# Three sums moved to transfers or to another place: the gates' T, the squares of h2, and the last pair of the down projection

## The chip, the cores and the metric

The kernel runs on one core of one Trainium2 chip. The metric is the device time of one execution in microseconds. Before the change the median of 3 runs is 2573.82 us (2573.16 to 2576.52).

The engines by the names of the profile: PE (TensorE, matrix products, with its weight loads PEld), DVE (VectorE), ACT (ScalarE), POOL (GpSimd) and SP (SyncE, which only issues transfers here). Each has its own queue of instructions and works them off in order; an instruction that waits holds all that stand behind it. SP, ACT and POOL also issue transfers (DMA).

## What is computed

One layer of a hybrid encoder on 512 tokens of 2048 numbers, in float32:

```python
u = rms_norm(h, mix_pre_g)
q, k, v, ca, cb, ga, gb = split(u @ w_in)
y_attn = neighbourhood_attention(q, k, v, rpb) @ w_attn_o
y_conv = conformer_conv(ca, cb, ...)
merged = sigmoid(ga) * y_attn + sigmoid(gb) * y_conv
h = h + rms_norm(merged @ w_out, mix_post_g)
u = rms_norm(h, ffn_pre_g)
gate, up = split(u @ w_gate_up)
f = (silu(gate) * up) @ w_down
h = h + rms_norm(f, ffn_post_g)
```

## The kernel before

**Tiles.** Everything is kept transposed: a tile has 128 features on the partitions and the 512 tokens along the row. The stream of 2048 features is 16 such tiles (KT = 16; HT = 8 is half of them). Tokens are also taken in halves, A and B, of 256. A tile of 128x512 float32 is 256 KB; most live in one pool of 66 slots (`slot`).

**Products.** TensorE's reduced float32 is used three times for one product: each operand is split into hi (a cast on ACT) and lo (what is left, a subtraction on DVE), and hi·lo, hi·hi and lo·hi are added (`gemm`, `interleaved`). Weights come in chunks of 512 KB: `wchunk` loads `raw_*` (SP, a pool of five buffers with the tag "raw"), casts it to `whi_*` (L126, ACT) and subtracts to `wlo_*` (L127, DVE), with three buffers each.

**Strassen pairs.** Most gates (gemms g2 to g15), the feed-forward's products (f5 and later) and a part of the down projection (d0 to d14) use the Winograd form of Strassen's algorithm: `strassen` takes two tiles of outputs at once, makes seven products of half size from four quarters of the weights (`g2q` and so on, also in the "raw" pool; `s1` has its own buffer and is summed by an accumulating transfer from POOL), and needs the activations as b11, b21, b22 and as sums T1 to T4 (`winograd_t`, `winograd_tt`). Its three sums x, y, z stand in PSUM banks: of `bank` (four) or `abank` (four more), in turn, by the parity of its last argument.

**Stage A, from g0 to g2** (L535 to L587). `u` is the normalized stream, 16 tiles as hi and lo. The gemm g0 makes the first two gates in four banks pg; it is a loop over c = 0 to 7 with one weight chunk each. In the same loop the operands of the Strassen pairs are made: SP copies halves of u's hi and lo into tiles b (six copies of 128 KB for each c, L552 and L553), `un` = hi + lo is summed (L547: one tile on POOL, one on DVE), `winograd_tt` makes `tt` from it on DVE, and `merged` splits tt (L148 a cast on ACT, L149 a subtraction on DVE). After the loop ACT takes four sigmoids of pg (L566), and the pairs i = 2 to 15 follow, where `strassen(..., i)` puts g2 on `bank`, that is on the banks of pg.

**Stage B, the second residual** (L666 to L734). `h2` makes the new stream tile by tile on DVE (L676, L677, L679); each tile is squared on ACT and added up by `sumsq` (L338), here on POOL. Meanwhile `interleaved` runs the gemm f0 on u_2, 8 chunks of 24 matmuls. Then `rstd` sums the squares over the partitions with small matmuls (r_s, L294), takes the power on POOL (L304), and `by_column` spreads the result over the partitions (r_b, L311); r3 is the copy of it on ACT (L699). A gemm of four chunks follows (two more columns of f0). All of the next stage on DVE starts from r3: L705 and L706 (the gated products of f0), L719 (the stream times r3) and the operands b and T of the following pairs. TensorE runs f1 in the meantime, 16 steps of 24 matmuls on halves (`plain`).

**Stage C, the down projection** (L829 to L855). Eight Strassen pairs; the results are joined on DVE (L284), multiplied by a row on POOL (L841) and added to y_d in DRAM by an accumulating transfer (L842). POOL's queue also issues the loads `ad*` (L758) of the activations that the last gemm, pd1, takes.

**The order.** A scheduler puts each engine's instructions in order when the kernel is built, by its own estimates and by the pools; `tc.keep_in_program_order` and `load_in_order` pin single ones.

Of the kernel before, what the change touches and what calls it, by code (L numbers as in the profile page):

```python
# [25 lines left out]
F32 = mybir.dt.float32  # L26
F32R = mybir.dt.float32r
AF = mybir.ActivationFunctionType
ALU = mybir.AluOpType
# [37 lines left out]
def hybrid_block(ctx: ExitStack, tc, xT, vecs, rpb, mask, w_c0, w_qk, w_v, w_gg, w_cg, w_ao, w_co, w_out, w_g0, w_gu, w_dn, outT):  # L67
# [264 lines left out]
    def sumsq(acc, x, name, last=False, eng=nc.vector):  # L332

        sq = slot(f"{name}_sq")
        nc.scalar.activation(sq, x, AF.Square)
        if acc is None or last:
            return (acc or []) + [sq]
        eng.tensor_tensor(out=acc[0], in0=acc[0], in1=sq, op=ALU.add)  # L338
        return acc

    def col(c, i):
# [73 lines left out]
            conv(i, pc[2 * i], pc[2 * i + 1])  # L415

    un = []

    def normalize(c):

        for k, t in enumerate(x_pair(c, f"xn{c}"), 2 * c):
            t2 = slot(f"un{k}")
            nc.vector.scalar_tensor_tensor(out=t2, in0=t, scalar=col(C_PRE, k), in1=r1, op0=ALU.mult, op1=ALU.mult)
            un.append(split(t2, f"un{k}"))

    rate = R_CONV
# [109 lines left out]
    pg = [bank(f"g0_{n}") for n in range(4)]  # L536
    for c in range(HT):
        hi, lo = wchunk(w_gg[c], f"g0_{c}")
        un = stp.tile([P, 2, NT], F32, tag="S", name=f"un{c}")
        for j, k in enumerate((c, c + HT)):  # L540
            ah, al = u[k]
            for n, ps in enumerate(pg):
                s = slice((j * 4 + n) * P, (j * 4 + n + 1) * P)
                nc.tensor.matmul(ps, hi[:, s], al, start=c + j == 0, stop=False)
                nc.tensor.matmul(ps, hi[:, s], ah, start=False, stop=False)
                nc.tensor.matmul(ps, lo[:, s], ah, start=False, stop=c + j == HT)
            (nc.gpsimd, nc.vector)[j].tensor_tensor(  # L547
                out=un[:, j], in0=ah.bitcast(F32), in1=al.bitcast(F32), op=ALU.add
            )
            blocks = [slot(f"b{j}{c}_{n}") for n in range(1 + j)]  # L550
            for t, cols in zip(blocks, (A, B)):
                nc.sync.dma_start(t[:, A], ah[:, cols].bitcast(F32))  # L552
                nc.sync.dma_start(t[:, B], al[:, cols].bitcast(F32))  # L553
# [19 lines left out]

    op = operands(b11, b2, t12, t34)
    for i in range(2, KT):
        c11, c12, c21, c22 = strassen(w_cg[2 * CT + i], w_cg[2 * CT + KT + i], op, f"g{i}", i)
        if i == KT - 1:
            ya = [load_ya(h) for h in range(YA_EARLY)]
        ga, gb = slot(f"ga{i}"), slot(f"gb{i}")
        joined(ga[:, A], c11)  # L580
        joined(ga[:, B], c12)
        nc.scalar.activation(ga, ga, AF.Sigmoid)
        nc.scalar.dma_start(g_d[i], ga)
        joined(gb[:, B], c22)
# [82 lines left out]
    a_d = dr.tile([FT, P, NT], F32, name="a_d")  # L667


    acc, u, w = None, [], []  # L670
    pf = [bank(f"f0_{n}") for n in range(4)]

    def h2(i, cols):
# [9 lines left out]
    for c in (*range(SPLIT), *range(HT)):  # L683
# [6 lines left out]
        for i in (2 * c, 2 * c + 1):  # L690
            h2(i, cols)
            if cols != A:
                nc.scalar.dma_start(h_d[i], f[i])
                acc = sumsq(acc, f[i], f"h{i}", last=i == KT - 1, eng=nc.gpsimd)
        if c == HT - 1:
            r = rstd(acc, D, "r3", pin=True)
        interleaved(pf, *w[c], u, c, cols)
    r3 = slot("r3")
    nc.scalar.copy(r3, by_column(r, "r3", pin=True))  # L699
    pf += [abank(f"f0_{n}") for n in range(4, 6)]  # L700
    gemm([(pf[4 + n], w_gu[n * FT + 2]) for n in range(2)], u, "f0")
    for j in range(3):
        t = stp.tile([P, 2, NT], F32, tag="S", name=f"sg{j}")
        t, up = t[:, 0], t[:, 1]
# [122 lines left out]


    op = operands(b11, b2, b_t12, b_t34)  # L829
    for o in range(0, KT, 2):  # L830
        if o == KT - 2:
            acts = [load(DN_S + k) for k in range(EARLY)]
# [1 line left out]
        c11, c12, c21, c22 = strassen(w0, w1, op, f"d{o}", o // 2)  # L834
        if o == KT - 2:
            acts += [load(DN_S + k) for k in range(EARLY, EARLY + MORE)]
        for i, (ca, cb) in enumerate(((c11, c12), (c21, c22))):
            t = slot(f"ys{o + i}")
            joined(t[:, A], ca)
            joined(t[:, B], cb)  # L840
            nc.gpsimd.tensor_tensor(out=t, in0=t, in1=irow, op=ALU.mult)  # L841
            nc.gpsimd.dma_start(y_d[o + i], t, accum_op=ALU.add)  # L842


    y = [None] * KT
# [1 line left out]
    for g in range(KT // 2 - 1):  # L847
        outs = [((bank, abank)[g % 2](f"pd1_{o}"), o) for o in (2 * g, 2 * g + 1)]
        for _, o in outs:
            y[o] = slot(f"y{o}")  # L850
            load_in_order(y[o], y_d[o])
        gemm([(ps, w_dn[o, :, DN_S * P :]) for ps, o in outs], acts, f"wd1_{g}", n=DN_R, more=lambda k: load(DN_S + k), pin=g < 2)
        for ps, o in outs:
            nc.vector.tensor_tensor(out=y[o], in0=ps, in1=y[o], op=ALU.add)  # L854
            acc = sumsq(acc, y[o], f"y{o}")  # L855
# [155 lines left out]
```

## The time and the profile before

| | before |
|---|---|
| median of 3 runs | 2573.82 us |
| the profiled execution, its own time | 2575.59 us |
| its span | 2573.8 us |
| granted TensorE clock, mean | 0.992 |
| PE busy | 2520.9 us, 98% |
| DVE busy | 1884.2 us, 73% |
| ACT busy | 1121.9 us, 44% |
| POOL busy | 355.8 us, 14% |
| bytes moved | 421.42 MB, mean 164 GB/s |

Times in the profile are microseconds from the start of the span. A row of the waits reads: the engine and line that waited, what it waited for, then the total, the number of times and the longest. A row in order of time reads: start, duration, engine, line, operation, output<-inputs, shape, how many together, and in brackets the idle time ahead with what ended it. A row of windows has the length of the window and then, for PE, PEld, DVE, ACT and POOL, the busy time with the number of instructions, and at its end the granted clock, the transfers' share of the 16 DMA engines, and GB/s. A row of groups has the busy time, the mean of one in ns, and the idle time ahead. A row of transfers has the issuing queue, the number, the size of each and the median time from issue to landing. The tile names lack their running number.

### The profile page before, as it was taken

The page shows a single profiled execution, that of the slowest core. Times are in us where ns is not written, and L with a number is a line of the kernel's source. Part 1 is how long each engine was busy: PE and PEld are TensorE (multiplying, and loading weights), DVE is VectorE, ACT ScalarE, POOL GpSimd, SP SyncE. Part 2 cuts the span into 40 slices and gives each one's busy share as a digit, 9 for nine tenths or more (in the row PEclk, how much of TensorE's full clock was granted, in tenths as well). Part 3 has the DMA queues.
Part 4 walks back from the last instruction along what each step waited for, and adds up shares of the span by engine and source line. Part 5 has one row for each costly group of instructions (what it writes and reads, how often), then busy time and mean ns, then how long its engine had stood idle before and what let it go on. Part 6 is the DMA issues. An engine that isn't in the chain of part 4 may idle for free.

```text
span 2573.8 us, 34661 instructions
## 1 busy us (share of the span) xinstructions
PE 2520.9 (98%) x13235; PEld 2163.8 (84%) x13235; DVE 1884.2 (73%) x2394; ACT 1121.9 (44%) x1644; POOL 355.8 (14%) x363
## 2 busy tenths in 40 slices
PE   9999999989999999998999999999999999989997
PEld 8888888878888888888898888888888878878887
DVE  5999896687775655338888888788888888863235
ACT  5223333355554422224455555555555565442222
POOL 0110222210000011003201111112120012230002
PEclk9999999999999999999999999999999999999999
DMA  6234323566667335224356665667666577773335
GB/s 208 93 126 150 109 92 108 156 209 185 183 194 245 136 127 193 95 98 150 117 152 172 178 182 172 176 204 213 195 193 195 168 244 198 185 243 112 115 114 164
DMA packets 143367, 421.42 MB, mean 164 GB/s; under 512 B 16608, under 2 KB 30048, under 8 KB 143200
## 3 DMA queue, kind: packets, MB, share of 16 engines
q1 hardware_dynamic: 106880, 326.42, 38.4%
q0 software_dynamic: 19040, 62.40, 11.8%
q10 hardware_dynamic: 17280, 30.38, 3.2%
q8 instruction: 104, 1.70, 0.3%
q14 instruction: 63, 0.52, 0.1%
HBM read 367.76 MB, written 45.09 MB: 160 GB/s over the span
## 4 chain that ended last, share of the span: by engine, by line
PE 91%; DVE 4%; DMA 2%; issue 2%; ACT 1%; POOL 1%; SPq 0%; DVEq 0%; ACTq 0%; POOLq 0%
PE f L246 19%; PE f L248 10%; PE g L246 7%; PE d L246 4%; PE g L248 3%; PE pd L172 3%; PE pd L176 3%; PE pd L175 3%; PE po L176 2%; PE po L172 2%; PE po L175 2%; PE qk L176 2%; PE qk L175 2%; PE qk L172 2%; PE py L172 2%; PE py L176 2%
## 5 line engine op out<-in xcount | busy, mean ns | idle before, releaser
L386 DVE SCALAR_TENSOR_TENSOR cv<-z,vec,cv 128x497 f32<-128x497 f32 (+14 forms) x240 | 190.8, 797 | 4.7
L127 DVE TENSOR_TENSOR wlo_wd<-raw_wd,whi_wd 128x1024 fp32r<-128x1024 f32 (+1 forms) x58 | 62.2, 1077 | 106.4 <-ACT whi_wd L126 105.2
L127 DVE TENSOR_TENSOR wlo_wo<-raw_wo,whi_wo 128x1024 fp32r<-128x1024 f32 x36 | 47.5, 1318 | 106.9 <-ACT whi_wo L126 106.8
L126 ACT CAST whi_wd<-raw_wd 128x1024 fp32r<-128x1024 f32 (+1 forms) x58 | 54.0, 934 | 157.5 <-PE pd L175 107.4
L126 ACT CAST whi_wo<-raw_wo 128x1024 fp32r<-128x1024 f32 x36 | 37.9, 1054 | 130.0 <-PE po L175 122.7
L304 POOL TENSOR_TENSOR r_r<-r_v,mhalf 128x2 f32<-128x2 f32 (+1 forms) x6 | 6.7, 1125 | 473.4 <-DVE r_v L302 473.4
L126 ACT CAST whi_y<-raw_y 128x1024 fp32r<-128x1024 f32 x32 | 33.5, 1052 | 83.5 <-PE py L175 79.4
L126 ACT CAST whi_qk<-raw_qk 128x1024 fp32r<-128x1024 f32 x32 | 33.6, 1051 | 77.1 <-PE qk L175 56.5
L127 DVE TENSOR_TENSOR wlo_qk<-raw_qk,whi_qk 128x1024 fp32r<-128x1024 f32 x32 | 40.5, 1264 | 32.1 <-ACT whi_qk L126 32.0
L627 DVE TENSOR_TENSOR gg<-py,gg 128x512 f32<-128x512 f32 x32 | 21.8, 690 | 55.7 <-PE py L176 55.7
L127 DVE TENSOR_TENSOR wlo_y<-raw_y,whi_y 128x1024 fp32r<-128x1024 f32 x32 | 53.3, 1670 | 12.5 <-ACT whi_y L126 11.3
L745 POOL TENSOR_TENSOR asum<-asum,asq 128x512 f32<-128x512 f32 x15 | 20.2, 1347 | 242.9 <-ACT asq L744 242.9
L172 PE MATMUL py<-ycl,whi_y 128*128 128x512 f32 x128 | 49.8, 389 | 0.0
L175 PE MATMUL py<-ych,whi_y 128*128 128x512 f32 x128 | 49.8, 389 | 0.0
L176 PE MATMUL py<-ych,wlo_y 128*128 128x512 f32 x128 | 49.8, 389 | 0.0
L788 ACT ACTIVATE sg<-sg 128x512 f32<-128x512 f32 x39 | 24.7, 634 | 51.6 <-DVE sg L284 51.6
L465 POOL TENSOR_TENSOR bm<-braw,msk 128x128 f32<-128x128 f32 x56 | 41.9, 781 | 15.9 <-DMA braw<-in_rpb 15.9
L769 POOL TENSOR_TENSOR an<-an,asum 128x512 f32<-128x512 f32 x16 | 27.8, 1735 | 102.6 <-DMA an<-a_d 100.6
L854 DVE TENSOR_TENSOR y<-pd,y 128x512 f32<-128x512 f32 x14 | 9.7, 692 | 41.4 <-PE pd L176 41.4
L841 POOL TENSOR_TENSOR ys<-ys,irow 128x512 f32<-128x512 f32 x16 | 27.4, 1715 | 85.6 <-DVE ys L284 42.7
L637 POOL TENSOR_TENSOR gg<-gg,gg 128x512 f32<-128x512 f32 x16 | 20.6, 1287 | 115.0 <-ACT whi_y L126 73.5
L156 PE MATMUL f<-b,wlo_f 128*128 128x256 f32 x128 | 36.3, 283 | 0.0
(3074 smaller groups left out, 8552.8 us busy)
## 6 DMA issues: line engine op xcount, KB each, us to landing
raw_wd<-in_w_dn SPq DMA_DIRECT2D x42, 512.0 KB, 3.6
raw_wo<-in_w_out SPq DMA_DIRECT2D x36, 512.0 KB, 3.8
raw_qk<-in_w_qk SPq DMA_DIRECT2D x32, 512.0 KB, 3.8
a_d<-sg ACTq DMA_DIRECT2D x44, 256.0 KB, 3.7
raw_v<-in_w_v SPq DMA_DIRECT2D x16, 512.0 KB, 3.7
raw_y<-in_w_ao SPq DMA_DIRECT2D x16, 512.0 KB, 3.7
gg<-g_d SPq DMA_DIRECT2D x32, 256.0 KB, 4.3
raw_y<-in_w_co SPq DMA_DIRECT2D x16, 512.0 KB, 3.6
```

The lines of the kernel that those rows point to most:

```text
L126: cast(hi[:, s], raw[:, s])
L127: nc.vector.tensor_tensor(out=lo[:, s], in0=raw[:, s], in1=hi[:, s].bitcast(F32), op=ALU.subtract)
L156: nc.tensor.matmul(o, lo, t[:, A], start=False, stop=last, skip_group_check=True)
L172: mmul = nc.tensor.matmul(ps, hi[:, s], al, start=first, stop=False)
L175: nc.tensor.matmul(ps, hi[:, s], ah, start=False, stop=False)
L176: nc.tensor.matmul(ps, lo[:, s], ah, start=False, stop=last)
L246: nc.tensor.matmul(ps, hi[:, ws[k]], t, start=first and k == 0, stop=False, skip_group_check=True)
L248: nc.tensor.matmul(ps[:, A], lo[:, ws[k]], t[:, A], start=False, stop=last and k == HT - 1, skip_group_check=True)
L386: nc.vector.scalar_tensor_tensor(out=a[:, to], in0=z[:, fr], scalar=col(C_WDW, i * CW + w), in1=a[:, to], op0=ALU.mult, op1=ALU.add)
L465: nc.gpsimd.tensor_tensor(out=bm[:, o + i - i0], in0=raw[:, :, i * BC : (i + 1) * BC], in1=msk[:, o + i - i0, None, :].broadcast_to([P, RO ...
L769: nc.gpsimd.tensor_tensor(out=t, in0=t, in1=arow, op=ALU.mult)
L841: nc.gpsimd.tensor_tensor(out=t, in0=t, in1=irow, op=ALU.mult)
```

## The change

1. `normalize` also writes each of the 16 normalized tiles to DRAM (`u_d`, from ACT's queue). In g0's loop the sums L547 go; `un` is loaded from u_d by SP, 512 KB for each c, in program order, into the "raw" pool of the weights.
2. The gates' Strassen pairs take the other parity (`i + 1`), so g2 stands on `abank` and not on the banks of pg.
3. The squares of h2 are no longer added on POOL. Those of i = 3 to 13 are added by accumulating transfers from POOL's queue onto those of i % 3, in three chains; with the last two there are five partial sums. `rstd` then has 20 small matmuls instead of 8. It stands behind the first chunk of the gemm that follows, `by_column` behind the second.
4. For the last Strassen pair of the down projection the multiply on POOL and the accumulating transfer stand behind the first gemm of pd1 in the code (`added`).

```diff
@@ normalize
+    u_d = dr.tile([KT, P, NT], F32, name="u_d")
...
             nc.vector.scalar_tensor_tensor(out=t2, in0=t, scalar=col(C_PRE, k), in1=r1, op0=ALU.mult, op1=ALU.mult)
+            nc.scalar.dma_start(u_d[k], t2)
             un.append(split(t2, f"un{k}"))
@@ g0
-        un = stp.tile([P, 2, NT], F32, tag="S", name=f"un{c}")
+        un = wp.tile([P, 2, NT], F32, tag="raw", name=f"un{c}", bufs=5)
+        load_in_order(un, u_d[c : c + HT + 1 : HT].rearrange("k p t -> p k t"))
...
-            (nc.gpsimd, nc.vector)[j].tensor_tensor(
-                out=un[:, j], in0=ah.bitcast(F32), in1=al.bitcast(F32), op=ALU.add
-            )
...
-        c11, c12, c21, c22 = strassen(w_cg[2 * CT + i], w_cg[2 * CT + KT + i], op, f"g{i}", i)
+        c11, c12, c21, c22 = strassen(w_cg[2 * CT + i], w_cg[2 * CT + KT + i], op, f"g{i}", i + 1)
@@ h2
-    acc, u, w = None, [], []
+    acc, u, w = [], [], []
...
                 nc.scalar.dma_start(h_d[i], f[i])
-                acc = sumsq(acc, f[i], f"h{i}", last=i == KT - 1, eng=nc.gpsimd)
-        if c == HT - 1:
-            r = rstd(acc, D, "r3", pin=True)
+
+                sq = slot(f"h{i}_sq")
+                nc.scalar.activation(sq, f[i], AF.Square)
+                if 3 <= i < KT - 2:
+                    nc.gpsimd.dma_start(acc[i % 3], sq, accum_op=ALU.add)
+                else:
+                    acc.append(sq)
         interleaved(pf, *w[c], u, c, cols)
-    r3 = slot("r3")
-    nc.scalar.copy(r3, by_column(r, "r3", pin=True))
+    r3, r = slot("r3"), []
     pf += [abank(f"f0_{n}") for n in range(4, 6)]
-    gemm([(pf[4 + n], w_gu[n * FT + 2]) for n in range(2)], u, "f0")
+    gemm(
+        [(pf[4 + n], w_gu[n * FT + 2]) for n in range(2)], u, "f0",
+        between=(
+            lambda: r.append(rstd(acc, D, "r3", pin=True)),
+            lambda: nc.scalar.copy(r3, by_column(r[0], "r3", pin=True)),
+        ),
+    )
@@ down projection
+    def added(ys):
+        for o, t in ys:
+            nc.gpsimd.tensor_tensor(out=t, in0=t, in1=irow, op=ALU.mult)
+            nc.gpsimd.dma_start(y_d[o], t, accum_op=ALU.add)
...
+        ys = []
         for i, (ca, cb) in enumerate(((c11, c12), (c21, c22))):
-            t = slot(f"ys{o + i}")
-            joined(t[:, A], ca)
-            joined(t[:, B], cb)
-            nc.gpsimd.tensor_tensor(out=t, in0=t, in1=irow, op=ALU.mult)
-            nc.gpsimd.dma_start(y_d[o + i], t, accum_op=ALU.add)
+            ys.append((o + i, slot(f"ys{o + i}")))
+            joined(ys[i][1][:, A], ca)
+            joined(ys[i][1][:, B], cb)
+        if o < KT - 2:
+            added(ys)
...
+        if g == 0:
+
+            added(ys)
```

Where the change moves instructions. First SP's queue in g0's loop (names: `raw_g0_5` is the weight chunk of c=5, `un5` the T sums' source of c=5, b14 and b05 the copies of c=4 and c=5). Before, the last weight chunks stand ahead of all copies:

```order
L125 DMA raw_g0_5_4327<-in_w_gg 128x1024
L125 DMA raw_g0_6_4385<-in_w_gg 128x1024
L125 DMA raw_g0_7_4443<-in_w_gg 128x1024
L226 DMA g2q_4519<-in_w_cg 128x1024
L259 DMA g2s1_4516<-in_w_cg 128x1024
L259 DMA g3s1_4700<-in_w_cg 128x1024
L552 DMA b00_0_4057<-un0h_1253 128x256
L553 DMA b00_0_4057<-un0l_1254 128x256
```

In the change:

```order
L552 DMA b14_1_4318<-un12h_1701 128x256
L553 DMA b14_1_4318<-un12l_1702 128x256
L125 DMA raw_g0_5_4339<-in_w_gg 128x1024
L91 DMA un5_4345<-u_d_497 128x2x512
L552 DMA b05_0_4359<-un5h_1512 128x256
L553 DMA b05_0_4359<-un5l_1513 128x256
L552 DMA b15_0_4374<-un13h_1708 128x256
L553 DMA b15_0_4374<-un13l_1709 128x256
L552 DMA b15_1_4375<-un13h_1708 128x256
L553 DMA b15_1_4375<-un13l_1709 128x256
L125 DMA raw_g0_6_4396<-in_w_gg 128x1024
L91 DMA un6_4402<-u_d_497 128x2x512
```

The loads raw_g of c = 5, 6 and 7 now stand behind all copies of the chunk before, each with the load of `un` behind it; all quarters of g2 stand behind the copies of c=7. On ACT the cast of the first quarter of g2, which stood among the casts of T of c=5, stands behind the four sigmoids.

Second, DVE around the first use of r3 (L705 before, L714 in the change; `wlo_f0_1_8` is the last chunk of f0's gemm, `wlo_f1_0` the first of f1). Before:

```order
L302 TENSOR_SCALAR r3_v_10118<-r3_s_10109 128x4
L127 TENSOR_TENSOR wlo_f0_0_0_10157<-raw_f0_0_0_10155,whi_f0_0_0_10156 128x1024
L127 TENSOR_TENSOR wlo_f0_1_0_10187<-raw_f0_1_0_10185,whi_f0_1_0_10186 128x1024
L127 TENSOR_TENSOR wlo_f0_0_8_10217<-raw_f0_0_8_10215,whi_f0_0_8_10216 128x1024
L705 TENSOR_TENSOR sg0_10275<-f0_0_9667,r3_10146 128x512
```

In the change:

```order
L127 TENSOR_TENSOR wlo_f0_0_8_10235<-raw_f0_0_8_10233,whi_f0_0_8_10234 128x1024
L302 TENSOR_SCALAR r3_v_10193<-r3_s_10172 128x4
L127 TENSOR_TENSOR wlo_f0_1_8_10265<-raw_f0_1_8_10263,whi_f0_1_8_10264 128x1024
L127 TENSOR_TENSOR wlo_f1_0_10317<-raw_f1_0_10315,whi_f1_0_10316 128x1024
L714 TENSOR_TENSOR sg0_10293<-f0_0_9676,r3_10139 128x512
```

Two subtractions of weights that stood behind the first uses of r3 stand ahead of them; r3's own first step, L302, stands behind three.

Third, POOL at the end of the down projection (`ys_20393` and `ys_20398` are the last pair before, `ys_20411` and `ys_20414` in the change; `ad_20469` and `ad_20483` are the load ad28 of an activation for pd1). Before:

```order
L841 TENSOR_TENSOR ys_20393<-ys_20393,irow 128x512
L842 DMA y_d<-ys_20393 128x512
L841 TENSOR_TENSOR ys_20398<-ys_20398,irow 128x512
L758 DMA ad_20469<-a_d 128x512
L842 DMA y_d<-ys_20398 128x512
L758 DMA ad_20475<-a_d 128x512
```

In the change:

```order
L842 TENSOR_TENSOR ys_20411<-ys_20411,irow 128x512
L843 DMA y_d<-ys_20411 128x512
L767 DMA ad_20483<-a_d 128x512
L842 TENSOR_TENSOR ys_20414<-ys_20414,irow 128x512
L843 DMA y_d<-ys_20414 128x512
L767 DMA ad_20489<-a_d 128x512
```

One load, ad28, moves ahead of the second multiply; the loads behind it keep their place.

More of the change, by code (lines that the diff above doesn't have):

```diff
@@ L330, in halves, with sumsq @@
         )
-    def sumsq(acc, x, name, last=False, eng=nc.vector):
+    def sumsq(acc, x, name, last=False):
         sq = slot(f"{name}_sq")
@@ L337, in sumsq @@
             return (acc or []) + [sq]
-        eng.tensor_tensor(out=acc[0], in0=acc[0], in1=sq, op=ALU.add)
+        nc.vector.tensor_tensor(out=acc[0], in0=acc[0], in1=sq, op=ALU.add)
         return acc
```

## The prediction

> **What bounds the kernel now.** I read first the page's shares and the chain of waits, then TensorE's waits over the whole run, then the three stages that the change touches, each by windows and by the order in time.
>
> ```profile
> PE 2520.9 (98%) x13235; PEld 2163.8 (84%) x13235; DVE 1884.2 (73%) x2394; ACT 1121.9 (44%) x1644; POOL 355.8 (14%) x363
> PE 91%; DVE 4%; DMA 2%; issue 2%; ACT 1%; POOL 1%; SPq 0%; DVEq 0%; ACTq 0%; POOLq 0%
> ...
> PE g L246 <- ACT gs L566: 8.0, 1, 8.0
> PE pd L172 <- DVE fa28l L137: 5.0, 1, 5.0
> PE f L190 <- DVE u_3l L679: 2.1, 1, 2.1
> PE g L246 <- ACT g2h L241: 1.6, 1, 1.6
> PE po L511 <- DVE ptl L509: 1.0, 1, 1.0
> ```
>
> TensorE is busy 2520.9 of a span of 2573.8 us and the change leaves out none of its large matmuls, so all it can win lies in about 53 us of idle time and in what a slow clock costs behind it. The three named waits lie in three stages: A, from the gemm g0 to the first Strassen pair g2 (485 to 560 us); B, f0 and h2 (1176 to 1310); C, the start of pd1 (2290).
>
> **Stage A: the sums T.** Before, the end of g0 is followed by an idle stretch:
>
> ```profile
> 524.99 0.39 PE L544 MATMUL g<-un7l,whi_g 128*128 128x512 f32 x1
> 530.20 0.39 PE L546 MATMUL g<-un15h,wlo_g 128*128 128x512 f32 x1
> ...
> 538.57 3.47 PE L246 MATMUL g<-b,g2h 128*128 128x512 f32 x8 [7.98 <-ACT gs L566]
> 550.29 2.00 PE L246 MATMUL g<-t,g2h 128*128 128x512 f32 x8
> ...
> 536.62 1.28 ACT L566 ACT_TABLE_LOAD   x1
> ...
> 500.00:505.00 5.00, 5.00 (x23) 4.14 (x23) 4.85 (x11) 2.45 (x6) 2.12 (x2) 1.00 1.05 226
> ```
>
> One chunk of g0 (24 matmuls) takes 5.45 us, so c=5 began at 524.99 - 2 x 5.45 = 514.1. The sigmoids start only at 537.9 because ScalarE's casts of T wait for VectorE, busy 4.85 of 5 us in a window of g0 (the third busy figure of its row). Then g2's first eight matmuls take 3.47 us, where eight at g0's spacing of 0.227 need 1.82: TensorE comes out of the pause slow, 1.6 us more. Gone by the edits: eight POOL sums, eight DVE sums of 0.69 us, the wait on pg's banks, and the 1.0 us at `ptl` (VectorE stood at its first sum there).
>
> But the loads of T stand in SP's queue and take weight buffers, and this moves raw_g of c=5 to 7 behind thirty copies of b:
>
> ```profile
> 472.24 0.33 SPq L125 DMA_DIRECT2D raw_g<-in_w_gg  x1
> ...
> 505.16 1.26 SPq L226 DMA_DIRECT2D g2q<-in_w_cg  x1
> 519.40 0.60 SPq L553 DMA_DIRECT2D b<-un12l  x1
> ...
> raw_g<-in_w_gg SPq DMA_DIRECT2D x8, 512.0 KB, 3.5
> g2q<-in_w_cg SPq DMA_DIRECT2D x4, 512.0 KB, 5.1
> g2s<-in_w_cg POOLq DMA_DIRECT2D x1, 512.0 KB, 7.3
> ```
>
> Before, raw_g of c=5 was issued at 472.2, 42 us ahead of its use. Now it follows the last copy of c=4. That one is issued by 520.0; three loads of g2q leave the queue ahead of it (1.3 us for the one at 505.16, some 0.7 for each of the two later) and one load of T joins (0.6): 517.9, and 517 with the lighter traffic. It lands as the g2q did among the copies, 5.1 us later, at 522; a cast of 1.05 us makes 523.2. TensorE, without the 1.0 us at ptl, wants it at 513.1: **it stands 10 us in the middle of g0**, and the slow clock behind it costs 1.6 us as above. Then c=5 ends at 523.2 + 5.45 + 1.6 = 530.2. The next weights follow eight issues apart (8 x 0.62 = 5.0, landing 527 and 532), in time; g0 ends at 541.1. The last sigmoid (0.54) and the cast of the first g2 quarter, now behind the sigmoids on ScalarE (1.05), give 542.8 for g2's start. From there its first three products took 11.7 us before (to the row at 550.29); without the 1.6 us of slow start and the idle 1.6 that the waits show, but with quarters that come a little late, I take 9.5: 552.3. **A = +2 us**. Bounds: SP issues the 24 copies of c=1 to 4 back to back at 0.6 from 498 (raw_g at 512.7), the weights land 3.5 later, c=5 starts at 517.3 and all that follows is 6 us earlier (-4); or raw_g at 520 and all later pairs of loads a further 1.5 us apart (+6). The first stall hides under nothing: TensorE has no other work in its queue.
>
> The sixteen writes of u are issues on ScalarE's queue in the v stage; they delay the casts and, with the later split, un15l by some 2 us:
>
> ```profile
> L137 DVE TENSOR_TENSOR un15l<-un,un15h x1: 685/685/685, 222.1 to 222.1; 128x512 fp32r<-128x512 f32 x1
> L453 PE MATMUL pv<-whi_v,un15l x8: 388/389/390, 225.0 to 270.5; 128*128 128x512 f32 x8
> ```
>
> It is ready at 222.8 and used at 225.0, a margin of 2.2: +0.2 (0 to 1).
>
> **Stage B: h2's squares.** What the fourteen POOL adds do shows on VectorE:
>
> ```profile
> 1180.00:1200.00 20.00, 16.98 (x121) 15.90 (x121) 19.24 (x32) 10.64 (x20) 8.36 (x6) 0.92 0.41 145
> 1200.00:1220.00 20.00, 16.10 (x68) 12.41 (x67) 20.00 (x20) 9.29 (x14) 11.09 (x7) 0.99 0.34 120
> 1220.00:1240.00 20.00, 18.80 (x90) 15.07 (x89) 15.57 (x17) 7.80 (x11) 8.84 (x5) 1.00 0.48 164
> ...
> L338 POOL TENSOR_TENSOR h_sq<-h_sq 128x512 f32<-128x512 f32 x14 | 25.6, 1825 | 21.2 <-ACT h_sq L335 20.8
> L676 DVE SCALAR_TENSOR_TENSOR f<-f,vec,r 128x512 f32<-128x512 f32 x12 | 11.8, 1004 | 0.0
> L679 DVE SCALAR_TENSOR_TENSOR u_13l<-f,vec,u_13h 128x512 fp32r<-128x512 f32 x1 | 1.8, 1777 | 0.0
> L679 DVE SCALAR_TENSOR_TENSOR u_9l<-f,vec,u_9h 128x512 fp32r<-128x512 f32 x1 | 0.7, 744 | 0.0
> ```
>
> VectorE is full (20.00 of 20) and TensorE idles 3.0 + 3.9 + 1.2 = 8.1 us, all of it for VectorE. The same instruction takes 1.78 us in one place and 0.74 in another; counted in the order in time, fourteen are longer by 1.05, 14.7 us in all, each beside a POOL add. The Trainium skill (SBUF — State Buffer, section SBUF: two separate sides) says why: a VectorE instruction with two SBUF inputs and a GpSimd one hold a shared port exclusively; the two rows agree. With the adds gone VectorE gains 14.7 us against 8.1 of stalls, so these go, and with them the slow clock (0.92 over 17 us, 1.4): 9.5. On TensorE:
>
> ```profile
> 1233.16 0.95 PE L294 MATMUL r_s<-ones,h_sq 128*128 128x1 f32 x8
> 1233.97 0.47 PE L187 MATMUL f<-u_14h,whi_f 128*128 128x512 f32 x1
> 1240.43 1.05 PE L311 MATMUL r_b<-ident,r_r 128*128 128x128 f32 x8
> 1241.24 0.48 PE L172 MATMUL f<-u_0l,whi_f 128*128 128x512 f32 x1
> 1242.85 0.68 DVE L705 TENSOR_TENSOR sg<-f,r 128x512 f32<-128x512 f32 x1
> 1249.19 1.21 DVE L127 TENSOR_TENSOR wlo_f<-raw_f,whi_f 128x1024 fp32r<-128x1024 f32 x1
> 1299.47 0.77 DVE L149 TENSOR_TENSOR b<-f,b 128x256 fp32r<-128x256 f32 x2
> 1309.19 2.00 PE L246 MATMUL f<-b,f5h 128*128 128x512 f32 x8
> ```
>
> Four small matmuls (eight records) take 0.81 us; r_s grows from 8 to 20 of them, 1.6 to 4.05, +2.4. The eleven accumulating transfers end long before r_s: a square comes every 2.6 us or so, a chain's next one after 7.8, and the like transfer above landed in 7.3. Interleaved part done: 1240.4 - 9.5 - 1.6 = 1229.3; first chunk 1234.8, r_s 1238.8, second chunk 1244.3, r_b 1245.1, two more chunks 1256.0, where f1 starts (before 1241.24 + 4 x 5.46 = 1263.1). So r3 comes **3.4 us later than now, though TensorE is 7.1 us earlier**, and all of VectorE's work in f1 hangs on r3. Two wlo (row at 1249.19, a pitch of 1.13 each) now stand ahead of the first use of r3 instead of behind it: VectorE in f1 is at 3.4 - 2.3 = +1.1 against before. Its last b ended at 1300.2 and would end at 1301.3; TensorE, at 2.88 us for each i, wants it at 1256.0 + 15 x 2.88 = 1299.2. So 2.1 of the 7.1 us come back as a stall: **B = -5 us**. Bounds: -7.1 if VectorE also loses its few gaps, -1.5 if it is held in f1 once more (ScalarE's r3 copy is now behind two weight casts).
>
> **Stage C: the last pair of the down projection.**
>
> ```profile
> 2291.52 0.70 POOL L758 DMA_DIRECT2D ad<-a_d  x1
> 2292.67 3.69 POOL L758 DMA_DIRECT2D ad<-a_d  x6
> 2298.70 0.80 PE L172 MATMUL pd<-fa28l,whi_wd 128*128 128x512 f32 x1 [4.96 <-DVE fa28l L137]
> 2300.77 0.80 PE L172 MATMUL pd<-fa29l,whi_wd 128*128 128x512 f32 x1 [0.43 <-DVE fa29l L137]
> ```
>
> The code moves; POOL's order hardly does: the first late load of `ad` goes up by one multiply (about 1.4 us), all others stay behind both multiplies and both y_d. fa28 comes earlier, fa29 does not, and TensorE then waits there: **C = 0** (-1.4 to +0.4). That is the edit that doesn't do what it says.
>
> **Sum.** +2 + 0.2 - 5 + 0 = -2.8 us against the profiled execution's own 2575.6 (its span and 1.8 around it). The median of the runs shown is 1.8 below it: 2573.8 - 2.8 = **2571.0**. About 0.2%, 5.1 us, is what a measurement of this kernel can tell from no change.
>
> **Rivals.** (1) *Faster: the weights of g0 come nearly in time.* The copies go at SP's pace (A = -4) and f1 keeps up (B = -7): 2573.8 - 11 = 2563. For it: SP issues every 0.6 us from 511 on. Against it: in the window quoted above the transfers' share is 1.05, all sixteen engines full, and then an issue takes over 1.2 us (row at 505.16). Chance 0.27. (2) *Slower: the accumulating transfers hold VectorE as the adds did, or come late behind it.* If all 9.5 us of stalls stay, the interleaved part ends at 1238.8, r3 at 1255, 13 us later than now less 2.3, and TensorE in f1 ends 8 to 9 us later: B = +8, in sum +10, 2584; it decides from about 5 us of kept stalls. The same page warns that descriptors which GpSimd writes for a transfer can starve while VectorE runs; no row here shows that, and the one g2s above, issued from POOL while VectorE was 4.85 of 5 busy, landed in 7.3. Chance 0.13. (3) *A costs what B wins:* raw_g at 520 or later (A = +6) with B = -5: 2575. Chance 0.17. (4) My forecast, 2571: 0.43.
>
> **The numbers.** Faster by over 0.2% (below 2568.7): nearly all of (1), a third of (4): 0.38. Slower (above 2579.0): (2) and small tails: 0.17. Within: 0.45. Range for 8 in 10: 2560 to 2581; the forecast's own 2566 to 2576.
>
> **What would show it.** After: a stall of about 10 us in g0 at c=5 that waits for whi_g, none over 3 us between g0 and g2; VectorE's instructions in h2 at 0.68 to 0.74 us, no stall of TensorE there; r_s at 4 us; new stalls of 2 us in f1 on b or wlo_f; fa28 at 3.5 and fa29 at 1.8 us. A c=5 without stall, or slow VectorE instructions in h2, makes the prediction wrong.

## The result and the profile after

| | before | after |
|---|---|---|
| median of 20 runs each, taken side by side | 2574.84 us (2569.53 to 2576.57) | 2578.09 us (2573.69 to 2583.69) |
| ratio after / before, 95% interval | | 1.0016 (1.0009 to 1.0023) |
| the profiled execution, its own time | 2575.59 us | 2581.3 us |
| its span | 2573.8 us | 2579.5 us |
| PE busy | 2520.9 us, 98% | 2529.9 us, 98% |
| DVE busy | 1884.2 us | 1858.6 us |
| POOL busy | 355.8 us | 324.7 us |
| bytes moved | 421.42 MB | 432.70 MB |

The ratio makes the change 4.1 us slower (0.0016 x 2574; interval 2.3 to 5.9). That is less than 0.2%, and its interval lies wholly above no change. The forecast was 2.8 us faster. VectorE has 25.6 us less to do and POOL 31.1 us less, and neither shortens the kernel.

TensorE's waits in the profile after (engine, line, what it waited for: total, times, longest):

```profile
PE g L547 <- ACT whi_g L126: 11.9, 1, 11.9
PE pd L172 <- DVE fa28l L137: 3.2, 1, 3.2
PE g L246 <- ACT g2h L241: 2.6, 1, 2.6
PE f L246 <- ACT f5h L241: 2.6, 1, 2.6
PE pd L172 <- DVE fa29l L137: 2.0, 1, 2.0
...
PE f L154 <- DVE b L149: 0.5, 2, 0.3
```

The waits that the edits aimed at are gone in stages A and B: `gs` (8.0), `ptl` (1.0) and all on `u_*` in h2. Two new ones have come: 11.9 us in the middle of g0, and 2.6 us on `f5h`, which is a Strassen pair behind f1.

**Stage A.** SP's queue in order of time, from the weights of c=4 on:

```profile
492.67 0.33 SPq L125 DMA_DIRECT2D raw_g<-in_w_gg  x1
...
494.38 0.53 SPq L552 DMA_DIRECT2D b<-un0h  x1
...
502.54 1.05 SPq L552 DMA_DIRECT2D b<-un9h  x1
503.65 1.64 SPq L553 DMA_DIRECT2D b<-un9l  x1
505.39 1.37 SPq L552 DMA_DIRECT2D b<-un9h  x1
...
521.02 0.60 SPq L553 DMA_DIRECT2D b<-un12l  x1
521.72 0.53 SPq L125 DMA_DIRECT2D raw_g<-in_w_gg  x1
...
526.71 0.54 SPq L125 DMA_DIRECT2D raw_g<-in_w_gg  x1
```

The weights of c=4 are issued at 492.67 and those of c=5 only at 521.72, behind all copies of c=0 to 4. TensorE ran dry at 515.1. The windows (length, then PE, PEld, DVE, ACT and POOL busy; granted clock, transfers' share, GB/s) and the rows of TensorE:

```profile
500.00:505.00 5.00, 5.00 (x24) 4.14 (x23) 4.90 (x12) 3.58 (x11) 2.42 (x3) 1.00 1.07 292
...
515.00:520.00 5.00, 0.12 (x1) 0.00 (x0) 0.00 (x0) 0.00 (x0) 0.00 (x0) 0.86 0.61 204
520.00:525.00 5.00, 0.00 (x0) 0.00 (x0) 0.00 (x0) 0.00 (x0) 0.00 (x0) 0.50 0.74 204
525.00:530.00 5.00, 3.00 (x7) 2.42 (x8) 2.97 (x6) 2.14 (x4) 0.00 (x0) 0.50 1.06 352
```

```profile
527.00 0.79 PE L547 MATMUL g<-un5l,whi_g 128*128 128x512 f32 x1 [11.88 <-ACT whi_g L126]
...
532.28 0.40 PE L547 MATMUL g<-un13l,whi_g 128*128 128x512 f32 x1
...
548.66 3.24 PE L246 MATMUL g<-b,g2h 128*128 128x512 f32 x8 [2.59 <-ACT g2h L241]
...
558.68 2.00 PE L246 MATMUL g<-t,g2h 128*128 128x512 f32 x8
```

Between 515.1 and 525 every compute engine is idle: ACT's cast waits for the load of raw_g, and VectorE and TensorE wait for that cast. All of it hangs on one transfer that stood in a queue. Behind the stall the clock is 0.50, and the first half of c=5, twelve matmuls, takes 532.28 - 527.00 = 5.28 us in place of 12 x 0.227 = 2.72. That is 2.6 us more. The last of the four rows is the product that began at 550.29 before: 8.4 us later, of which 2.1 had gathered before stage A (1.4 at the start, 0.7 in the v stage). So A is +6.3 here.

**Stage B.** The same windows as before over h2, and what follows it on TensorE:

```profile
1180.00:1200.00 20.00, 20.00 (x161) 19.53 (x161) 19.23 (x40) 12.63 (x24) 3.49 (x4) 1.00 0.62 188
1200.00:1220.00 20.00, 20.00 (x90) 16.57 (x89) 20.00 (x29) 14.16 (x22) 6.55 (x8) 1.00 1.06 276
...
1238.00:1240.00 2.00, 2.00 (x15) 2.00 (x15) 0.00 (x0) 0.00 (x0) 0.00 (x0) 0.71 0.00 0
1240.00:1242.00 2.00, 2.00 (x11) 2.00 (x11) 0.00 (x0) 0.00 (x0) 0.00 (x0) 0.50 0.00 0
```

```profile
1236.37 6.28 PE L294 MATMUL r_s<-ones,h_sq 128*128 128x1 f32 x40
...
1308.46 2.00 PE L246 MATMUL f<-b,f5h 128*128 128x512 f32 x8
1309.73 1.28 DVE L759 TENSOR_TENSOR sg<-f,sg 128x512 f32<-128x512 f32 x2
1310.93 1.21 DVE L231 TENSOR_TENSOR f5s<-f5s,f5q 128x1024 f32<-128x1024 f32 x1
1312.90 1.03 ACT L241 CAST f5h<-f5s 128x1024 fp32r<-128x1024 f32 x1
1313.98 3.64 PE L246 MATMUL f<-t,f5h 128*128 128x512 f32 x8 [2.58 <-ACT f5h L241]
```

TensorE is busy 20.00 of 20 us where it was 16.98 and 16.10. The first f5 product starts 0.7 us earlier than before (1308.46 against 1309.19), though TensorE had entered h2 4.3 us later. Then two things give most of this back. The 40 records of r_s take 6.3 us, and in the windows over them the clock falls to 0.50 while TensorE is shown as busy without a gap. And the second f5 product waits 2.6 us and runs 3.64 instead of 2.00.

### The profile page after: what moved, and what is told of

The parts are those of the page before. It is cut to its first block, busy times and chain, and to the rows that moved or that the text cites. A ratio compares the mean times of both kernels' runs of the same rounds, so it can differ in the third digit from the quotient of the medians.

```text
span 2579.5 us, 34740 instructions
## 1 busy us (share of the span) xinstructions
PE 2529.9 (98%) x13259; PEld 2172.3 (84%) x13259; DVE 1858.6 (72%) x2386; ACT 1122.1 (44%) x1644; POOL 324.7 (13%) x352
## 2 busy tenths in 40 slices
DMA packets 149431, 432.70 MB, mean 168 GB/s; under 512 B 17168, under 2 KB 30608, under 8 KB 149264
## 4 chain that ended last, share of the span: by engine, by line
PE 84%; DVE 7%; issue 3%; DMA 3%; ACT 1%; POOL 1%; SPq 1%; ACTq 0%; DVEq 0%; POOLq 0%
PE f L246 19%; PE f L248 10%; PE g L246 7%; PE g L248 3%; PE pd L176 3%; PE pd L172 3%; PE pd L175 3%; PE d L246 3%; PE po L172 2%; PE po L176 2%; PE po L175 2%; PE qk L176 2%; PE qk L175 2%; PE qk L172 2%; PE py L172 2%
## 5 line engine op out<-in xcount | busy, mean ns | idle before, releaser
L154 PE MATMUL f<-b,whi_f 128*128 128x256 f32 x128 | 36.4, 285 | 0.5 <-DVE b L149 0.5
L155 PE MATMUL f<-b,whi_f 128*128 128x256 f32 x128 | 36.2, 283 | 0.0
```

The lines of the kernel that those rows point to most:

```text
L154: nc.tensor.matmul(o, hi, t[:, B], start=first, stop=False, skip_group_check=True)
L155: nc.tensor.matmul(o, hi, t[:, A], start=False, stop=False, skip_group_check=True)
```

## The experiments

Each was timed beside the kernel before on the same chip. A ratio is turned into microseconds by 2574. "By the alignment" means that the start of each matmul in one trace is set against the start of the same matmul in another, here the first profile of before where no other is named; a change of that difference is what a stage won or lost.

### The four edits, one at a time

```diff
# 1 alone: T read back
+            nc.scalar.dma_start(u_d[k], t2)
...
+        un = wp.tile([P, 2, NT], F32, tag="raw", name=f"un{c}", bufs=5)
+        load_in_order(un, u_d[c : c + HT + 1 : HT].rearrange("k p t -> p k t"))
# 2 alone: the other banks
-        c11, c12, c21, c22 = strassen(w_cg[2 * CT + i], w_cg[2 * CT + KT + i], op, f"g{i}", i)
+        c11, c12, c21, c22 = strassen(w_cg[2 * CT + i], w_cg[2 * CT + KT + i], op, f"g{i}", i + 1)
# 3 alone: h2's squares by transfers, r_s and by_column between the chunks
+                if 3 <= i < KT - 2:
+                    nc.gpsimd.dma_start(acc[i % 3], sq, accum_op=ALU.add)
...
+            lambda: r.append(rstd(acc, D, "r3", pin=True)),
# 4 alone: the last pair of the down projection
+        if o < KT - 2:
+            added(ys)
```

Expected of edit 1: 

> Before with the first edit alone: u written to DRAM, T's source read back into the weights' buffers. Theory (order of SP's queue): the stall of about 12 us at c=5 of g0 and the slow clock behind it come from this edit alone; the stage from 490 to 560 us ends 6 to 8 us later than before, the v stage 0.5 to 1 later, in all +6 to +9 us. Rival (the stall needs the other edits' traffic or order): stall at c=5 under 6 us and the time within 3 us of before. A gain of 3 to 4 us in the layer norm (800 to 835 us) here would put that gain down to this edit and not to the banks.

Expected of edit 2: 

> Before with the gates' Strassen pairs on the other banks alone. Theory (the change's gain of 4.3 us between 800 and 835 us comes from the banks, since g15 no longer shares them with the layer norm's sums): -3 to -5 us there, and 0 to -3 us between g0 and g2, in all -3 to -8. Rival (that gain comes from the earlier or later traffic of the first edit): 0 in the layer norm, in all 0 to -3.

Expected of edit 3: 

> Before with the squares of h2 added by transfers alone, r3 in the following gemm. Theory (all that stage B gave and lost is this edit's own): 13 us won in h2, 4 to 6 lost at r_s, 1 in f1, 4 at the second product of f5, whose weight sum stands behind the products of f1 on VectorE; in all -2 to +1. Rival (the stall at f5 is an accident of the whole change's order): no stall over 1 us at f5, in all -4 to -7.

Expected of edit 4: 

> Before with the last pair's multiply and accumulating transfer later in the code alone. Theory (the 2 us that stage C lost are this edit's: fa28 earlier, fa29 and the following later, and a slow clock behind two stalls): +1.5 to +2.5. Rival (they are run-to-run differences of the transfers in that stage): within 1 us of before.

| edit alone | median, us | ratio (95%) | in us |
|---|---|---|---|
| 1, T read back | 2580.78 | 1.0032 (1.0020 to 1.0045) | +8.2 |
| 2, banks | 2573.70 | 1.0002 (0.9993 to 1.0010) | +0.5 |
| 3, squares | 2570.04 | 0.9985 (0.9976 to 0.9994) | -3.9 |
| 4, last pair | 2574.49 | 1.0000 (0.9991 to 1.0009) | 0.0 |

The sum is +4.8, against +4.1 for the whole change: within the intervals the edits add up, and the loss is edit 1's. Edit 1 came out as expected; edits 2 and 4 did nothing, where -3 to -8 and +1.5 to +2.5 had been expected from the first trace of the whole change, and edit 3 won more than its -2 to +1. Its row of waits is that of the whole change, 11.8 us on `whi_g` in g0, with the weights of c=5 issued at 520.44.

Edit 2 shows well how a wait moves. TensorE's rows with the other banks only:

```profile
530.32 1.75 PE L246 MATMUL g<-b,g2h 128*128 128x512 f32 x7
...
542.47 3.54 PE L246 MATMUL g<-t,g2h 128*128 128x512 f32 x8 [8.39 <-ACT g2h L241]
```

g2's first product starts 8.25 us earlier (538.57 before) and the second 2.1 us earlier (544.60 before). Its quarter of the weights is cast on ScalarE behind the sigmoids of g0, which still wait. The banks were not the last thing that g2 waited for.

Edit 3 wins what h2 idled. From the start of h2 to the end of its interleaved part TensorE gains 12.0 us, in this profile as in the whole change's. The forecast's 9.5 added the idle time that the profile shows to the slow clock. Matmul by matmul, each of the eight stalls had cost about 0.3 more than its idle time (the one on u_12l: 0.9 shown, 1.2 by the alignment), in part because a matmul is shown as busy for 0.39 us where the next one starts after 0.23. r_s puts the matmuls behind it 4.3 us back here (6.0 in the whole change), the clock falls to 0.61 and 0.54 in the two windows behind it, and the second f5 product waits 2.5 us: the two ways in which it is lost again are those of the whole change. The eleven accumulating transfers landed after 7.3 us by their median, and VectorE's instructions beside them keep their length. The group of the whole change that took 1004 ns in the mean before:

```profile
L676 DVE SCALAR_TENSOR_TENSOR f<-f,vec,r 128x512 f32<-128x512 f32 x12 | 8.7, 742 | 0.0
```

### T in buffers of its own

If the raw buffers are what pushes the weights of c=5 behind the copies, `un` in the pool that it had before must leave them where they were.

```diff
# edit 1, but
-        un = wp.tile([P, 2, NT], F32, tag="raw", name=f"un{c}", bufs=5)
+        un = stp.tile([P, 2, NT], F32, tag="S", name=f"un{c}")
```

> Before with the first edit alone, but T's source read back into the buffers that held the sums before, not into the weights'. All weight chunks of g0 then stand ahead of the copies in SP's queue, as in the kernel before; bytes moved and VectorE's sums left out are the same as in the first edit. Theory (the edit's +7 us come from where the weight chunks stand in SP's queue): no stall at c=5; what is left of the 8.0 us between g0 and g2 is 1 to 5 us, since VectorE has 5.5 us less to do there; in all -4 to -8 us against before. Rival (the read-back's bytes or u's writes cost the time): a stall in g0 stays, or the time stays at +3 us or more.

Measured: 2588.79 us, ratio 1.0066 (1.0053 to 1.0079), +17 us. The stall at c=5 is gone, as the cause demands, and the time is worse: the pool has two buffers, each load of T waits until the sums from an earlier one are done, and while it waits it holds SP, with all copies behind it. TensorE's largest wait, and the first and the last of T's eight loads:

```profile
PE g L246 <- ACT gs L566: 25.1, 1, 25.1
```

```profile
492.61 0.39 SPq L91 DMA_DIRECT2D un<-u_d  x1
...
547.07 0.38 SPq L91 DMA_DIRECT2D un<-u_d  x1
```

The last operand of g2 is loaded at 547, where g2 had begun at 538.57. So the cause of the stall is confirmed, and the cure has a price that was not foreseen (-4 to -8 had been expected): the queue is the resource, whether weights or sums stand behind what waits in it.

### The weights, then T too, from another queue

```diff
# edit 1, and the weights of c=5 to 7 from POOL's queue
+        queue = nc.gpsimd if c >= 5 else nc.sync
+        hi, lo = wchunk(w_gg[c], f"g0_{c}", queue=queue)
# and, in the second kernel, T of c=4 to 7 as well
+        tc.keep_in_program_order((nc.gpsimd if c >= 4 else nc.sync).dma_start(un, u_d[c : c + HT + 1 : HT].rearrange("k p t -> p k t")))
```

> The first edit alone, with one thing moved: the weight chunks of g0 for c = 5 to 7 are issued from POOL's queue, which is idle there, into the same buffers. T's loads and the copies stay on SP. Theory (the stall at c=5 is the chunk's place behind the copies in SP's queue): the chunk is issued as soon as its buffer is free, some 10 us earlier, and the stall falls from 11.8 us to under 2; T's loads of c = 5 to 7 are still behind the copies, so 6 to 10 us of idle time between g0 and g2 come back; in all 0 to +4 against before instead of +8. Rival (the buffer, held by T's source, is what the chunk waits for): the stall stays at 8 us or more.

> As the kernel beside it, and T's loads of c = 4 to 7 from POOL's queue as well. Theory (T's lateness is the second thing that SP's queue costs): no stall over 2 us in g0, under 5 us of idle time between g0 and g2; -2 to -6 against before. Rival (the transfers themselves are the limit, 16 engines full from 497 to 545 us): the idle time only moves, and the time stays within 3 us of before or is longer.

Weights alone: 2578.57 us, 1.0017 (1.0009 to 1.0026), +4.4. The 11.8 us at c=5 are gone (0.2 is left), and a new stall stands one chunk later:

```profile
516.13 0.50 PE L550 MATMUL g<-un5h,wlo_g 128*128 128x512 f32 x1 [0.23 <-DVE wlo_g L127]
...
532.51 0.79 PE L550 MATMUL g<-un6h,wlo_g 128*128 128x512 f32 x1 [9.64 <-DVE wlo_g L127]
```

VectorE works in order: the subtraction of c=6's weights stands behind sums T whose `un` is still behind the copies on SP. With T on POOL's queue too: 2574.30 us, 0.9998 (0.9989 to 1.0007), +-0. Nothing stalls inside g0 any more, and the wait is back where it was before the change, at g2, but on another thing:

```profile
541.68 3.78 PE L246 MATMUL g<-b,g2h 128*128 128x512 f32 x8 [8.49 <-DMA b<-un15h]
```

```profile
500.00:510.00 10.00, 10.00 (x46) 8.27 (x45) 6.63 (x15) 3.51 (x9) 5.72 (x8) 1.00 1.02 303
510.00:520.00 10.00, 10.00 (x46) 8.29 (x45) 6.00 (x14) 4.13 (x10) 0.56 (x1) 1.00 1.04 347
```

VectorE is busy 6.63 and 6.00 of 10 us, where it had been 4.85 of 5; the transfers' share is 1.02 and 1.04. In the second window the transfers that POOL issued, weights and T, take 83.7% of it and SP's copies only 20.6%. From 520 to 530 VectorE is at 9.65 of 10 again, with the T that came late, but what g2 waits for is the last copy. The copies of b, held up beside T and the weights, are the bound. Edit 1 at its best trades 8 us of waiting for VectorE for 8 us of waiting for transfers.

### What takes back the squares' gain

Two parts of edit 3 were changed, one at a time: the order behind f1, and the number of small matmuls.

```diff
# edit 3, and the products sg3 and sg4 later in the scheduler's order
+    with tc.high_priority(offset=-200):
         for j in range(2):
             t = slot(f"sg{3 + j}")
# edit 3, and three partial sums in place of five: 12 small matmuls
-                if 3 <= i < KT - 2:
+                if i >= 3:
```

> The third edit alone, with the products of f1 (activation and multiply of tiles 3 and 4) given a lower priority, so that f5's weight sum stands ahead of them on VectorE. Theory (the 2.5 us stall at f5's second product and the slow clock behind it come from that order): the stall goes, and with it 2.5 to 4.2 us; against before -6.5 to -8.5. Rival (the weight sum is late in any order because VectorE itself is behind): the stall stays within 1 us of 2.5 and the time is that of the third edit alone, -3.9.

> The third edit alone, but with the squares of tiles 14 and 15 in the chains too: three partial sums, 12 small matmuls in place of 20. Theory (the block of small matmuls costs by its length, 0.21 us each, and by the clock, which falls to 0.5 when such a block passes 3 to 4 us): 12 take 2.6 us, the clock stays near 1.0 behind them, TensorE is 3 to 4 us earlier there and r3 as much; against the third edit alone -2 to -4 us. Rival (VectorE in f1 and f5's stall decide, r_s is covered): within 1 us of the third edit alone. Second rival (the last accumulations come too late): TensorE waits at r_s and the time is longer than the third edit's.

sg later: 2568.08 us, 0.9981 (0.9972 to 0.9990). The row of the second f5 product, where edit 3 alone has 3.56 us behind a wait of 2.55:

```profile
1302.70 2.12 PE L246 MATMUL f<-t,f5h 128*128 128x512 f32 x8 [0.45 <-ACT f5h L241]
```

The stall and the slow product go: 2.1 us less waiting and 1.4 of a faster product, and behind them TensorE is 3.7 us better off by the alignment. Over the whole of stage B only 2.0 of that are left, because the 40 records of r_s put TensorE 5.4 us back in this trace, where it was 4.3 with edit 3 alone, and leave more of the slow clock behind them (2.2, where it was 1.7). In the runs it is 1 us by the ratios (0.9981 against 0.9985; -6.5 to -8.5 against before had been expected, and it is -4.9) and the intervals overlap, so that the cause is shown by the rows, and its worth in the time is not settled.

Twelve matmuls: 2566.44 us, 0.9974 (0.9963 to 0.9986), 2.8 us under edit 3 alone by the ratios, whose intervals overlap too.

```profile
1228.55 2.73 PE L294 MATMUL r_s<-ones,h_sq 128*128 128x1 f32 x24
```

```profile
1228.00:1230.00 2.00, 2.00 (x18) 1.88 (x17) 0.00 (x0) 1.04 (x1) 0.00 (x0) 1.00 0.21 82
1230.00:1232.00 2.00, 2.00 (x16) 1.85 (x16) 0.69 (x2) 0.00 (x0) 0.44 (x1) 1.00 0.00 0
```

24 records in 2.7 us leave the clock at 1.00 here; behind or within 40 it fell in all three traces that have them. r_s is shorter by 1.8 against edit 3 alone, and the slow clock behind it (1.7) is gone. That the shorter block is safe does not follow: of the two kernels below that also have 24 records, the first keeps its clock at 1.00, and the second, the best of all, loses it behind a block of the same 2.7 us and pays 1.7 us. Its rows:

```profile
1226.97 2.73 PE L294 MATMUL r_s<-ones,h_sq 128*128 128x1 f32 x24
...
1230.00:1232.00 2.00, 2.00 (x8) 1.61 (x7) 1.05 (x1) 0.00 (x0) 1.94 (x1) 0.71 0.00 0
1232.00:1234.00 2.00, 2.00 (x6) 1.56 (x5) 0.00 (x0) 0.00 (x0) 0.00 (x0) 0.50 0.77 262
```

In the kernel with twelve matmuls alone the second f5 product, in the old order, waits 1.6 us and takes 2.14.

### Together

Edits 1, 2 and 3 with twelve small matmuls and sg later, first with `un` in its pool of two, then with weights and T from POOL's queue:

```diff
# first
+        un = stp.tile([P, 2, NT], F32, tag="S", name=f"un{c}")
+        load_in_order(un, u_d[c : c + HT + 1 : HT].rearrange("k p t -> p k t"))
# second
+        hi, lo = wchunk(w_gg[c], f"g0_{c}", queue=queue)
+        un = wp.tile([P, 2, NT], F32, tag="raw", name=f"un{c}", bufs=5)
+        tc.keep_in_program_order((nc.gpsimd if c >= 4 else nc.sync).dma_start(un, u_d[c : c + HT + 1 : HT].rearrange("k p t -> p k t")))
# both
+                if i >= 3:
...
+    with tc.high_priority(offset=-200):
```

> The changed kernel without its fourth edit, with T's source in its own buffers, 12 small matmuls and the products of f1 at a lower priority. If the theories of the three kernels beside it hold and add up: the sum of their gains, -12 to -18 us against before. Rival (VectorE or the transfers take back what one part wins): less than -8.

> The first three edits, with weights and T's loads from POOL's queue, 12 small matmuls for the squares, and the products of f1 at a lower priority. If the parts add up: stage A -3 to -7 (now without the wait on pg's banks), stage B -9 to -12, in all -10 to -18. Rival (something is given back later): -6 or less.

The first: 2579.22 us, 1.0020 (1.0011 to 1.0029). g2 no longer waits for its banks but for its copies, in three places (`b` from un5l, un6l and un7l: 6.0, 8.1 and 5.4 us), and TensorE is 19 us late behind it; the mended stage B wins 9.3 back. Of the -12 to -18 that had been expected nothing came. The second: 2564.84 us (2560.70 to 2566.13), 0.9960 (0.9946 to 0.9974), **10.3 us faster than before** and the best of all kernels here. Its stage A is only 1.7 us better than before's, with 7.4 us in two waits on g2h, where -3 to -7 had been expected; most of the gain is stage B's (7.7 by the alignment, though its block of small matmuls loses the clock).

### Before once more

> The kernel before, unchanged, profiled once more. Theory (the waits at ya4l, 2.1 us, and the 3 to 4 us that all five kernels win between 820 and 880 us, as well as the 2 to 3 us that they lose at 2300 us, are differences from run to run in the landing of transfers and in the granted clock): against the first profile of before, shifts of 2 to 4 us at just these two places and under 0.5 us elsewhere. Rival (they come from the edits): no shift over 1 us there.

One more profile of the kernel before itself, 2578.21 us, aligned with the first one matmul by matmul, tells which differences no edit makes. It stands 1.4 us later from the start on, gains 3.6 us between 800 and 880 (a stage of loads in which the change touches nothing), loses 1.4 more in h2 and 2.4 more in stage C, and waits differently there. Its rows of stage C:

```profile
PE pd L172 <- DVE fa29l L137: 2.3, 1, 2.3
PE pd L172 <- DVE fa24l L137: 2.3, 1, 2.3
...
PE pd L172 <- DVE fa28l L137: 1.8, 1, 1.8
```

The first profile had 5.0 at fa28 and 0.8 at fa24. So the 4.1 us that the whole change's trace gains in the stage of loads, and the 2.1 that it loses in stage C, need no edit to explain them. The stalls of 8.0 on `gs` and 1.6 on `g2h` are the same in both profiles of before, but the slow clock behind the first costs 1.1 us more in the second: the products with g2l take 1.91 there, and took 1.11.

```profile
539.99 3.78 PE L246 MATMUL g<-b,g2h 128*128 128x512 f32 x8 [7.97 <-ACT gs L566]
543.57 1.91 PE L248 MATMUL g<-b,g2l 128*128 128x256 f32 x8
```

Stage A can be read from one trace to about 1 us, stage C cannot.

## Why the prediction was wrong

**The step that failed is the size of term A.** It was put at +2 us. Edit 1 alone measures +8.2 (5.1 to 11.6) in the runs; the traces show +6.3 for the whole change and +6.7 for edit 1 alone in stage A (1.1 less each against the second profile of before), and 0.7 in the v stage, where 0.2 had been taken. The mechanism was right to the chunk: c=5's weights behind the copies, a stall in g0 on `whi_g`, none over 3 us between g0 and g2. The terms were each too small:

| of term A | predicted | the whole change | edit 1 alone |
|---|---|---|---|
| raw_g of c=5 issued | 517 | 521.72 | 520.44 |
| the stall at c=5 | 10 | 11.9 | 11.8 |
| slow clock behind it | 1.6 | 2.6 | 2.9 |
| wait on g2h ahead of g2's first product | 1.6 (a sigmoid and a cast) | 2.6 | 2.8 |
| g2's first eight matmuls | 1.9 (3.47 - 1.6) | 3.24 | 3.07 |

Three choices made it. The issue time, 517, was the end of c=4's copies before the change, less 0.4 to 1.3 us for each load of g2q that leaves the queue. But the stretch did not shrink with its number of issues. The first copy of c=0, before:

```profile
492.25 0.53 SPq L552 DMA_DIRECT2D b<-un0h  x1
```

From there to the last copy of c=4 (519.40) SP took 27.15 us; in the whole change it took 26.64 (494.38 to 521.02). Three loads of g2q, 2.7 us by the sum, were gone, one load of T (0.4) had joined, and 0.5 us was won. The three rows after 502 above show where it went: they took 1.05 to 1.64 us each, with the transfers' share at 1.07 in that window, and the next two took 1.13 and 1.17. From 505 to 510 it is not the copies that fill the engines but what POOL issued, above all the two accumulating transfers g2s and g3s. By queues (POOL's is the software one; packets, MB, share), first 505 to 510, then 515 to 520, where the copies are alone:

```profile
q0 software_dynamic: 277, 1.00, 86.3%
q1 hardware_dynamic: 295, 0.28, 18.9%
...
q1 hardware_dynamic: 1118, 1.02, 61.0%
```

Alone, the copies leave SP every 0.64 us and take 0.61 of the engines. A full share by itself does not make the issues long: from 525 to 530 it is 1.06 without POOL's transfers, and the copies issued there take 0.47 to 0.77. That POOL's two transfers hold SP up from 502 to 509 is what the rows suggest; no run took them away. The first copy stood 2.1 us later than before, which is the later start of the whole stage: it arose in the kernel ahead of stage A, so it delays TensorE's demand for c=5 as well (515.1, 513.1 in the working) and lengthens no stall. From the issue to the first matmul of c=5 it was 5.3 us where 6.2 had been taken. Second, the slow clock was taken from g2's start before, behind 8 us of idle, where part of the eight matmuls already ran at full speed; behind 11.9 us the clock was 0.50 for twelve matmuls. One trace was too few for that price: the same 8 us cost 2.7 in the second profile of before. The Trainium skill (TensorE: Matmul & The Clock Gate, section What's actually happening) states that the clock is halved after at least one idle window of about 3.4 us and comes back after at least one busy window as long; the clock of 0.50 behind 11.9 us, and the 5.3 us from the first matmul to full speed, agree. Third, the working had 1.6 us between g0 and g2 and 9.5 for g2's first three products, at the full clock: g2 waited 2.6 us, started slowly a second time, and the three took 10.0 (548.66 to 558.68). The rival "A costs what B wins", A at +6 and chance 0.17, described the case that came, on the place of the issue (520 or later) as well; it set B at -5.

**B was right in sum, by errors that cancel; that is luck.** Predicted -5; edit 3 alone measures -3.9 (-6.2 to -1.5). The single profiles show less, -2.3 for edit 3 and -0.7 for the whole change; against the second profile of before, which takes 1.4 us longer in this stage, they show -3.7 and -2.1, and r_s was slower in the whole change's. Along the way:

- The stalls of h2: 12.0 us won, 9.5 predicted, for the reason given with edit 3.
- r3: the working has it 3.4 us later than before. Its own terms give 3.8 (r_b done at 1245.1, and at 1241.24 before), by which B would have been -4.6.
- r_s: 4.3 us alone and 6.0 in the whole change where 4.05 was predicted, and 1.6 to 1.7 of slow clock behind it (2.2 with sg late), which no step had.
- The stalls on b in f1: 1.1 us, 2.1 predicted. f1's end came 5.1 us earlier in the whole change and 6.7 with edit 3 alone, measured from the start of h2, against 5 predicted.
- The wait on f5h behind it, 2.6 us and 1.6 of slow product, was missed. The new order of VectorE puts two products of f1's results (L759) ahead of the sum f5s (L231) that the next product needs; before, L231 ran at 1302.49, inside f1. L759 can run only after f1's end, so f5s and its cast come behind it. Nothing in the working asked whether an instruction that moved ahead waits for something later.

**Edits 2 and 4 cost nothing, as predicted.** Edit 2 moved its wait on by one product. Of edit 4, 1.0000 (0.9991 to 1.0009) bears out C = 0; the waits at fa28 and fa29 (3.2 and 2.0, predicted 3.5 and 1.8) come near, but the second profile of before shows that their own spread is as large.

**The rivals.** "The weights come nearly in time" fell with the issue at 521.7. "The accumulating transfers hold VectorE" fell too: L676 takes 742 ns in place of 1004, all stalls of h2 are gone, and the transfers landed in 7.2 us, as the g2s had. (The g2s was weaker evidence than the prediction took it for: it was issued at 498.4, in a pause of VectorE from 496.4 to 498.9, and not in the window of 4.85 of 5.) So the shared port told of in the prediction costs VectorE time beside POOL's additions, and not beside these transfers.

**What stays open.** Why r_s costs 4.3 us in one profile and 6.0 in the other was not tried; the clock fell behind it in the one and inside it in the other. Nor is it known why a block of 24 keeps the clock in two traces and loses it in a third, or what makes SP's issues long beside POOL's transfers. The sizes of 1 to 3 us within stage B come from ratios whose intervals overlap.

## What to carry to other kernels

A sum that is moved from a compute engine to transfers is paid for in the queue that issues them and in the buffers that they take: write down that queue in order, find what was pushed behind it, and ask what the next bound will be once the engine is free. An instruction that moves forward in an in-order engine brings its own wait with it; look at what it waits for, not only at its length. Where the terms are of 2 to 8 us, a kernel for each edit separates them, and a second profile of the same kernel tells which differences belong to none.

## What the runs showed of the hardware that was not expected

- A block of small matmuls can cost the clock as a pause does. 40 records of 128x1 keep TensorE busy in the profile for 4.5 to 6.3 us, and the granted clock falls to 0.50 to 0.54 in or behind them, in three traces of three; 24 records in 2.7 us leave it at 1.00 in two traces and are followed by 0.71 and 0.50 in the third. The price behind the block was 1.6 to 2.2 us.
- Copies of 128 KB within SBUF, alone, go at the pace of the queue that issues them: one every 0.64 us from SP, 204 GB/s, with the sixteen transfer engines at 0.61 (515 to 520), each landed 2.0 to 2.1 us after its issue. Beside accumulating transfers from POOL (86.3% of the engines from 505 to 510) the copies issued there landed after 4.7 to 8.0 us. With the weights and T on POOL's queue, g2 waits 8.5 us for the last of them.
- Accumulating transfers of 256 KB issued from POOL landed in 7.2 us by their median (3.4 to 9.8) beside a VectorE that was busy 20.00 of 20 us, without slowing it.
